# A macaron encoder layer on one core: how the normed input rows are scaled and turned

## The chip, the core and the metric

The kernel runs on one core of a Trainium2 chip. The metric is the device time of one launch in microseconds (us). Engines are named as in the profile: PE (TensorE, with PEld its weight loads), DVE (VectorE), ACT (ScalarE), POOL (GpSimd), SP (SyncE, which here only issues DMAs; ACT issues some too, shown as ACTq).

## The reference, cut to what matters

One layer over 1024 prompt tokens and 32 sample tokens, 1024 features each. The change lies in the first lines, the first feed-forward block:

```
def rms_norm(x, g):
    y = xf * lax.rsqrt(jnp.mean(xf * xf, axis=-1, keepdims=True) + EPS)
    return (y * g.astype(jnp.float32)).astype(x.dtype)

def swiglu(x, w_in, w_out):
    a, b = jnp.split(x @ w_in, 2, axis=-1)
    return (jax.nn.silu(a) * b) @ w_out

x = x + 0.5 * swiglu(rms_norm(x, ffn1_norm), ffn1_w_in, ffn1_w_out)
```

Behind it come the mixing block (stick-breaking attention beside an HGRN2 scan, between two projections) and a second feed-forward block. `d_ff` is 2816, so `ffn1_w_in` is 1024 x 5632. All of it is float32.

## The kernel before, in words

**Products.** A float32 product runs as three products of rounded halves (h and l of each side; `PASSES`, L431). The feed-forward matmuls use a fast scheme of seven block products in place of eight: the normed input, turned so that features lie on partitions, is cut into blocks (`B11`, `B12`, `B21`, `B22`: feature half by token half), and sums of them (`T1` to `T4`) are made. Each block or sum is split into h (ACT, L158) and l (DVE, L159). Tokens come in two column parts, c = 0 (256 columns, operands named `...0h`, `...0l`) and c = 1 (272, in tiles `B11s`, `T2s`). Weights come in 22 column groups j: `load_a(j)` fetches 512 KB (`wraw`, two buffers, so that a load waits until the l of the group two places earlier is written), `load_b(j)` another (`braw`), and S1 to S4 are sums of both.

**The first stage, where the change is.** Nine row tiles (`Tile`: eight of 128 prompt tokens, number 8 with the 32 sample tokens) are fetched in token order (`xt`). For each, `factor` squares the row on ACT with a running sum (L791) and makes the factor r on POOL in two small instructions (L793, L794); before, DVE then makes a 128x128 diagonal `dg` of r (L796). `normed` multiplies the row by that diagonal on PE, eight matmuls per tile (L808), which turns and scales it at once, and DVE multiplies with the gain `g1` out of the PSUM bank (L819, into `xn`). `raw` turns the unscaled row as well (eight transposes with the identity, L806), ACT copies it out (L831), and it goes to DRAM for the residual.

**Order of the work.** Each engine runs its instructions in the order in which a scheduler laid them down at build time from the order of the code and its own estimates; waits are on semaphores. `early_products` runs the products `A11*B11` and `A12*B21` of the groups j = 0 to 5, since they need only two blocks. Its order is j = 0 and 1 for c = 0, then j = 0 and 1 for c = 1, then j = 2, 3, 4, 5 with both parts. After step n it calls `amid(n)`, in which further rows are normed and saved, the remaining operands made (`prep_rest`) and at last the second weights started (`start_weights`: load_a(0) again, load_b(0), the sums on POOL, L479 to L482, and their splits). Then `first_products` runs the other five products of j = 0 (S2*T2 first, in the trace `T20h,S2h`), then j = 1, and so on; partial results of the early products come back from DRAM (`p`, `gt`), and DVE adds the banks up (L552).

Of the kernel before, what the change touches and what calls it, by code (L numbers as in the profile page):

```python
# [45 lines left out]
def first_consts(g, pool, w):  # L46
    nc = g.nc
    tmp = g.wp.tile([P, CW[1]], F32, name="idtmp", tag="xp", bufs=3)[:, 0:P]
    make_identity(nc, tmp)
# [4 lines left out]
    nc.vector.memset(ones, 1.0)
    g.ones = ones[:, 0:1].broadcast_to([P, P])
    g.eps = pool.tile([P, 1], F32, name="eps")
    nc.vector.memset(g.eps, EPS)
    g.g1 = col(g, pool, "g1", w["ffn1_norm"].rearrange("o (c p) -> p (o c)", p=P), KC)
# [717 lines left out]
class Tile:  # L776


    def __init__(self, g, w, pool, psp, tt):
# [4 lines left out]
        tag, bufs = ("xt", 8) if tt < 8 else ("st", 6)
        self.xt = pool.tile([P, D], F32, name="xt", tag=tag, bufs=bufs)
        g.landed = nc.sync.dma_start(self.xt[0:R], src)

    def factor(self, spare):
        g, nc, pool, R = self.g, self.g.nc, self.pool, self.R
        ss = pool.tile([P, 1], F32, name="ss", tag="ss", bufs=3)  # L790
        nc.scalar.activation(spare[0:R], self.xt[0:R], AF.Square, accum_out=ss[0:R])  # L791
        r = pool.tile([P, 1], F32, name="r", tag="r", bufs=3)
        nc.gpsimd.tensor_scalar(out=r[0:R], in0=ss[0:R], scalar1=1.0 / D, scalar2=EPS, op0=ALU.mult, op1=ALU.add)  # L793
        g.power = nc.gpsimd.tensor_tensor(out=r[0:R], in0=r[0:R], in1=g.mh[0:R], op=ALU.pow)  # L794
        self.dg = pool.tile([P, P], F32, name="dg", tag="dg", bufs=4)
        nc.vector.tensor_scalar(out=self.dg[0:R, 0:R], in0=g.ident[0:R, 0:R], scalar1=r[0:R, 0:1], scalar2=None,  # L796
                                op0=ALU.mult)

    def turned(self, h, m):

        nc, R = self.g.nc, self.R
        pn = self.psp.tile([P, 4, P], F32, name="bk", tag="bk", bufs=8)
        for k in range(4):
            src = self.xt[0:R, (4 * h + k) * P:(4 * h + k + 1) * P]
            if m is None:
                nc.tensor.transpose(pn[:, k, 0:R], src, self.g.ident[0:R, 0:R])  # L806
            else:
                nc.tensor.matmul(pn[:, k, 0:R], src, m[0:R, 0:R], start=True, stop=True)  # L808
# [828 lines left out]
def tile_layer(ctx: ExitStack, tc: tile.TileContext, *aps):  # L1637
# [38 lines left out]
    first_consts(g, const, w)  # L1676
# [342 lines left out]
```

## Time and profile before

| | |
|---|---|
| median of three runs | 2153.51 us (2150.92 to 2155.53) |
| profiled execution | 2152.1 us, span of the trace 2150.4 us |
| PE busy | 2106.0 us, 98% of the span |
| DVE, ACT, POOL busy | 1473.9, 938.7, 593.3 us |
| mean granted TensorE clock | 0.998 |

A timeline row reads: start in us, duration in us, engine, line, operation, tile written from tiles read, shapes, how many instructions the row merges, and in brackets how long the engine sat idle before it and what released it. A row of a stage table reads: stretch, its length, busy time (and count) of each engine, PEclk (the TensorE clock that the records show as granted, 1.00 is full), DMA share and GB/s. A DMA row on SPq or ACTq is its issue, not its transfer. L numbers are lines of the kernel before.

### The profile page before, as it was taken

The numbers are of one execution on the slowest core, as the hardware profiler recorded it, in microseconds if no ns is written. First come the engines' busy times: TensorE is split into PE (matmuls) and PEld (weight loads), VectorE is DVE, ScalarE is ACT, GpSimd is POOL, SyncE is SP. The second block draws the span as 40 slices with busy tenths as digits, with TensorE's granted clock in tenths as the row PEclk, the third lists the DMA queues.
The fourth block names the chain that finished last, engine by engine and source line by source line (L and its number), as shares of the span: only waits on it lengthen the run. The fifth ranks groups of instructions, "written<-read, shape, count | busy, mean of one in ns | idle before, by whom it ended". The sixth has DMA issues, their size and how long they took to land.

```text
span 2150.4 us, 41462 instructions
## 1 busy us (share of the span) xinstructions
PE 2106.0 (98%) x16331; PEld 2055.2 (96%) x16331; DVE 1473.9 (69%) x2559; ACT 938.7 (44%) x1830; POOL 593.3 (28%) x873
## 2 busy tenths in 40 slices
PE   7999999999999999999999999999999999999999
PEld 7999999999999999989899898999999999999998
DVE  5877666564678658778778689559777666645775
ACT  6433333233446555555554565236323233334444
POOL 1355544441000110311311311021555354320000
PEclk9999999999999999999999999999999999999999
DMA  7665555547535320120121122464775555566343
GB/s 231 189 211 173 154 175 158 164 137 269 201 124 168 117 62 21 44 71 21 51 63 29 56 66 91 145 196 148 237 219 172 165 166 164 166 222 237 120 148 126
DMA packets 327364, 305.12 MB, mean 142 GB/s; under 512 B 26432, under 2 KB 283200, under 8 KB 327168
## 3 DMA queue, kind: packets, MB, share of 16 engines
q1 hardware_dynamic: 258016, 262.59, 37.8%
q10 hardware_dynamic: 68672, 38.25, 6.2%
q8 instruction: 128, 2.10, 0.4%
q0 software_dynamic: 480, 1.62, 0.2%
q14 instruction: 68, 0.56, 0.1%
HBM read 207.37 MB, written 95.03 MB: 141 GB/s over the span
## 4 chain that ended last, share of the span: by engine, by line
PE 85%; DVE 5%; DMA 4%; issue 2%; POOL 2%; ACT 2%; ACTq 0%; DVEq 0%; SPq 0%; POOLq 0%
PE bk L431 36%; PE bk L752 19%; PE pp L891 14%; PE ps L1529 2%; PE pl L1400 2%; PE av L1167 1%; PE pt L1148 1%; DMA oraw<-in_ffn_w_out_dram 1%; PE z L1203 1%; PE bk L808 1%; PE ps L1556 1%; PE z L1202 1%; DVE t L1061 1%; DMA pd<-e 1%; DMA p<-pd 1%
## 5 line engine op out<-in xcount | busy, mean ns | idle before, releaser
L752 PE MATMUL bk<-tl,wh 128*128 128x256 f32 x1144 | 325.0, 285 | 1.1 <-DVE tl L709 1.1
L752 PE MATMUL bk<-th,wl 128*128 128x256 f32 x1144 | 324.4, 284 | 0.5 <-DVE wl L697 0.5
L752 PE MATMUL bk<-th,wh 128*128 128x256 f32 x1144 | 323.0, 284 | 0.7 <-ACT th L708 0.7
L891 PE MATMUL pp<-xs_a,wh 128*128 128x384 f32 (+1 forms) x1008 | 258.5, 338 | 0.0
L752 PEld LDWEIGHTS bk<-tl,wh 128*128 128x128 f32 x1144 | 215.2, 188 | 1.8 <-DVE tl L709 1.8
L752 PEld LDWEIGHTS bk<-th,wl 128*128 128x128 f32 x1144 | 215.2, 188 | 1.0 <-DVE wl L697 0.7
L752 PEld LDWEIGHTS bk<-th,wh 128*128 128x128 f32 x1144 | 214.4, 188 | 1.2 <-ACT th L708 1.0
L891 PEld LDWEIGHTS pp<-xs_a,wh 128*128 128x128 f32 x1008 | 168.6, 189 | 6.1 <-issue 4.1
L891 PE MATMUL pp<-xs_a,wl 128*128 128x384 f32 (+1 forms) x504 | 163.9, 325 | 0.0
L586 POOL TENSOR_TENSOR gt<-gt,b 128x256 f32<-128x256 f32 x88 | 74.4, 846 | 314.4 <-ACT gt L585 310.3
L697 DVE SCALAR_TENSOR_TENSOR wl<-oraw,wh 128x1024 fp32r<-128x1024 f32 x78 | 89.8, 1152 | 95.8 <-ACT wh L696 95.7
L696 ACT ACTIVATE wh<-oraw 128x1024 fp32r<-128x1024 f32 x78 | 77.7, 996 | 135.4 <-PE bk L752 115.9
L585 ACT ACTIVATE gt<-gt 128x256 f32<-128x256 f32 x88 | 37.3, 424 | 224.2 <-DVE gt L552 224.0
L431 PE MATMUL bk<-ops_a,wh 128*128 128x256 f32 (+1 forms) x704 | 131.6, 287 | 2.5 <-ACT e L411 2.5
L159 DVE TENSOR_TENSOR wl<-wraw,wh 128x512 fp32r<-128x512 f32 (+2 forms) x126 | 110.8, 894 | 33.6 <-ACT wh L158 32.1
L158 ACT ACTIVATE wh<-wraw 128x512 fp32r<-128x512 f32 (+2 forms) x126 | 89.5, 731 | 88.6 <-PE pp L891 25.2
L431 PEld LDWEIGHTS bk<-ops_a,wh 128*128 128x128 f32 x704 | 110.0, 190 | 3.4 <-ACT e L411 3.4
L590 POOL TENSOR_TENSOR gt<-gt,b 128x256 f32<-128x256 f32 x88 | 89.4, 1016 | 80.2 <-DVE b L552 67.8
L431 PE MATMUL bk<-ops_a,wl 128*128 128x272 f32 (+1 forms) x352 | 100.4, 286 | 0.3 <-DVE wl L159 0.3
L552 DVE TENSOR_TENSOR gt<-bk,p 128x256 f32<-128x256 f32 (+1 forms) x60 | 26.0, 433 | 105.9 <-PE bk L431 99.9
L891 PEld LDWEIGHTS pp<-xs_a,wl 128*128 128x128 f32 x504 | 94.7, 188 | 0.1
L1059 ACT ACTIVATE t<-z,minus 128x128 f32<-128x128 f32 (+2 forms) x96 | 55.4, 578 | 63.2 <-PE z L1205 48.9
(446 smaller groups left out, 6701.7 us busy)
## 6 DMA issues: line engine op xcount, KB each, us to landing
wraw<-in_ffn_w_in_dram SPq DMA_DIRECT2D x58, 512.0 KB, 4.3
oraw<-in_ffn_w_out_dram SPq DMA_DIRECT2D x94, 256.0 KB, 4.5
sd<-osum SPq DMA_DIRECT2D x44, 512.0 KB, 3.2
gd<-gt SPq DMA_DIRECT2D x42, 528.0 KB, 5.0
braw<-in_ffn_w_in_dram ACTq DMA_DIRECT2D x42, 512.0 KB, 4.4
oraw<-sd SPq DMA_DIRECT2D x40, 512.0 KB, 3.8
oraw<-in_ffn_w_out_dram SPq DMA_DIRECT2D x30, 512.0 KB, 3.5
wraw<-in_w_in_dram SPq DMA_DIRECT2D x28, 512.0 KB, 3.6
```

Source lines behind the costliest of these rows:

```text
L158: nc.scalar.activation(hi, src, AF.Copy)
L159: return nc.vector.tensor_tensor(out=lo, in0=src, in1=hi, op=ALU.subtract)
L431: mm = g.nc.tensor.matmul(ps, wt[x][:, kk, :], xt[y][:, kk, :], start=(first and kk == 0 and n == 0), stop=(kk == HK - 1 and n == len(PASS ...
L586: nc.gpsimd.tensor_tensor(out=gt[:, 1, cc], in0=gt[:, 1, cc], in1=s["b2"], op=ALU.mult)
L590: last = nc.gpsimd.tensor_tensor(out=gt[:, 0, cc], in0=gt[:, 0, cc], in1=s["b1"], op=ALU.mult)
L696: nc.scalar.activation(h, r, AF.Copy, scale=0.5)
L697: nc.vector.scalar_tensor_tensor(out=l, in0=r, scalar=0.5, in1=h, op0=ALU.mult, op1=ALU.subtract)
L752: nc.tensor.matmul(ps, wt[a][:, d * P:(d + 1) * P], xt[b][:, cols(c)], start=(k == 0 and n == 0), stop=(k == FH - 1 and n == len(PASSES) - 1))
L891: g.filler = nc.tensor.matmul(ps[:, 0:gw(n)], wt[a][:, k, :], xs(b, k)[:, gs(n)], start=(k == 0 and j == 0), stop=(k == KC - 1 and j == le ...
L1059: nc.scalar.activation(a, z, AF.Sigmoid, scale=minus)
L1400: nc.tensor.matmul(pl[0:rows, c, 0:hl].rearrange("p (b m) -> p b m", m=m_), k[:, cs(b, c)][:, 0:rows], qr, start=True, stop=True)
L1529: nc.tensor.matmul(ps[:, 0:w], wt[a][:, k, :], xs(b, c)[:, gs(n)], start=(k == 0 and i == 0), stop=(k == 5 and i == len(PASSES) - 1))
```

## The change

`factor` now multiplies the row itself by r, in two halves of 512 columns, into a new tile `xr`: on ACT for rows 1 and 3, on DVE for rows 0 and 8, on POOL for rows 2, 4, 5, 6 and 7. `normed` turns `xr` with the identity, as `raw` turns `xt`. The diagonals go. Only rows 0 and 1 are turned ahead of the first products; the turns of rows 2, 3 and 8, of 4 and 5, and of 6 and 7 move behind steps 0, 2 and 3. The gain `g1` is fetched behind two row tiles and the first weights, no longer first. `load_a(1)` moves ahead of the first factors in the code.

```
-        self.dg = pool.tile([P, P], F32, name="dg", tag="dg", bufs=4)
-        nc.vector.tensor_scalar(out=self.dg[0:R, 0:R], in0=g.ident[0:R, 0:R], scalar1=r[0:R, 0:1], scalar2=None,
-                                op0=ALU.mult)
+        self.xr = pool.tile([P, D], F32, name="xr", tag="st", bufs=6)
+        for h in range(2):
+            cs = slice(HD * h, HD * h + HD)
+            out, src = self.xr[0:R, cs], self.xt[0:R, cs]
+            if self.tt in (1, 3):
+                nc.scalar.activation(out, src, AF.Copy, scale=r[0:R, 0:1])
+            else:
+                eng = nc.vector if self.tt in (0, 8) else nc.gpsimd
+                eng.tensor_scalar(out=out, in0=src, scalar1=r[0:R, 0:1], scalar2=None, op0=ALU.mult)
...
-            if m is None:
-                nc.tensor.transpose(pn[:, k, 0:R], src, self.g.ident[0:R, 0:R])
-            else:
-                nc.tensor.matmul(pn[:, k, 0:R], src, m[0:R, 0:R], start=True, stop=True)
+            nc.tensor.transpose(pn[:, k, 0:R], rows[0:R, (4 * h + k) * P:(4 * h + k + 1) * P], self.g.ident[0:R, 0:R])
...
     def amid(n):
-        if n == 1:
+        if n == 0:
+            norm_rows(2, 3, 8)
+            factor_rows(4, 5)
+        elif n == 1:
             prep_first(g, None, None, None, xs[1], xns[1])
             save_rows(8, 0, 1)
+            factor_rows(6, 7)
+        elif n == 2:
+            norm_rows(4, 5)
+            save_rows(2)
         elif n == 3:
-            save_rows(2)
-            norm_rows(4, 5)
+            prep_rest(g, None, None, None, xs[0], xns[0])
+            norm_rows(6, 7)
             save_rows(3, 4, 5)
-            for tt in (6, 7):
-                rows[tt].factor(spare)
-            prep_rest(g, None, None, None, xs[0], xns[0])
-            for tt in (6, 7):
-                rows[tt].normed(xns)
+        elif n == 4:
             save_rows(6, 7)
...
     wts.load_a(0)
+    g.g1 = col(g, const, "g1", w["ffn1_norm"].rearrange("o (c p) -> p (o c)", p=P), KC)
     fetch_rows(2, 3, 8)
+    wts.load_a(1)
+    factor_rows(0, 1)
     norm_rows(0, 1)
     wts.split_a(0)
     prep_first(g, None, None, None, xs[0], xns[0])
-    wts.load_a(1)
-    norm_rows(2, 3, 8)
+    factor_rows(2, 3, 8)
```

The scheduler lays the instructions down anew. Line numbers of the changed kernel differ: its L789 is L791 of before, L791 and L792 are L793 and L794, L157 and L158 are L158 and L159, L451 and L459 are L452 and L460, L551 is L552, L430 is L431; its L798 and L801 are the new multiplications.

ACT at the start of the program, before: squares of the rows (`T40h` is only scratch there), the first weights' h, and the h of the first two blocks.

```order
2 L791 ACTIVATE T40h,ss<-xt 128x1024 x2
3 L158 ACTIVATE wh<-wraw 128x1024
4 L791 ACTIVATE T40h,ss<-xt 128x1024 x2
5 L791 ACTIVATE T40h,ss<-xt 32x1024
6 L158 ACTIVATE B110h<-xn_104 128x1024
7 L158 ACTIVATE B210h<-xn_104 128x1024
8 L158 ACTIVATE wh<-wraw 128x1024
```

ACT at the same place, changed:

```order
2 L789 ACTIVATE T40h,ss<-xt 128x1024 x2
3 L157 ACTIVATE wh<-wraw 128x1024
4 L798 ACTIVATE xr<-xt,r 128x512 x2
5 L789 ACTIVATE T40h,ss<-xt 128x1024 x2
6 L798 ACTIVATE xr<-xt,r 128x512
7 L157 ACTIVATE B110h<-xn_88 128x1024
8 L157 ACTIVATE B210h<-xn_88 128x1024
9 L798 ACTIVATE xr<-xt,r 128x512
10 L789 ACTIVATE T40h,ss<-xt 32x1024
```

The multiplications of row 1 stand ahead of the squares of rows 2 and 3, and the first half of row 3's stands ahead of `B110h`. The factor that it waits for comes from POOL, which at the start of the changed kernel runs this row (rows 0 and 1, then row 2 with its multiplications, then row 3, then row 8):

```order
9 L791 TENSOR_SCALAR r<-ss 128x1 x2
10 L792 TENSOR_TENSOR r<-r,mh 128x1 x2
11 L791 TENSOR_SCALAR r<-ss 128x1
12 L792 TENSOR_TENSOR r<-r,mh 128x1
13 L801 TENSOR_SCALAR xr<-xt,r 128x512 x2
14 L791 TENSOR_SCALAR r<-ss 128x1
15 L792 TENSOR_TENSOR r<-r,mh 128x1
16 L791 TENSOR_SCALAR r<-ss 32x1
17 L792 TENSOR_TENSOR r<-r,mh 32x1
```

Row 3's factor now stands behind both multiplications of row 2; before, POOL had only the pairs of small instructions.

SP's DMA issues from the third weight load on, before: three more weight loads (j = 3, 4, 5), then `braw` of j = 0, then three (j = 0 again, 1, 2).

```order
8 L452 DMA wraw<-in_ffn_w_in_dram 128x8x128
9 L786 DMA xt<-in_x_prompt_dram 128x1024 x2
10 L452 DMA wraw<-in_ffn_w_in_dram 128x8x128 x3
11 L460 DMA braw<-in_ffn_w_in_dram 128x8x128
12 L452 DMA wraw<-in_ffn_w_in_dram 128x8x128 x3
```

The same place, changed:

```order
8 L451 DMA wraw<-in_ffn_w_in_dram 128x8x128
9 L784 DMA xt<-in_x_prompt_dram 128x1024 x2
10 L451 DMA wraw<-in_ffn_w_in_dram 128x8x128 x5
11 L459 DMA braw<-in_ffn_w_in_dram 128x8x128
12 L451 DMA wraw<-in_ffn_w_in_dram 128x8x128
```

`braw` of j = 0 now stands behind five loads, the last two of which are those of j = 0 and 1 for the second time.

DVE at the end of j = 0 in `first_products`, before (`u` is the first addition for j = 1 and needs the `p` that comes from DRAM; `S4l` is a weight of j = 1):

```order
82 L552 TENSOR_TENSOR b_1137<-bk,p_1117 128x272
83 L159 TENSOR_TENSOR A22l<-braw,A22h 128x512
84 L552 TENSOR_TENSOR gt_953<-bk,u_1090 128x272
85 L552 TENSOR_TENSOR u_1185<-bk,p_1167 128x256
86 L159 TENSOR_TENSOR S4l<-rS_1030,S4h 128x512
```

And changed:

```order
73 L551 TENSOR_TENSOR b_1146<-bk,p_1126 128x272
74 L158 TENSOR_TENSOR A22l<-braw,A22h 128x512
75 L551 TENSOR_TENSOR gt_962<-bk,u_1099 128x272
76 L158 TENSOR_TENSOR S4l<-rS_1039,S4h 128x512
77 L551 TENSOR_TENSOR u_1194<-bk,p_1176 128x256
```

`S4l` has come ahead of the `u` that waits for `p`. From j = 4 of `first_products` on, all engines run the same instructions in the same order in both kernels.

More of the change, by code (lines that the diff above doesn't have):

```diff
@@ L57, in first_consts @@
     nc.vector.memset(g.eps, EPS)
-    g.g1 = col(g, pool, "g1", w["ffn1_norm"].rearrange("o (c p) -> p (o c)", p=P), KC)
     g.r = pool.tile([P, T], F32, name="rstd")
@@ L783, in __init__ @@
         R = self.R
-        tag, bufs = ("xt", 8) if tt < 8 else ("st", 6)
-        self.xt = pool.tile([P, D], F32, name="xt", tag=tag, bufs=bufs)
+        self.xt = pool.tile([P, D], F32, name="xt", tag="xt", bufs=9)
         g.landed = nc.sync.dma_start(self.xt[0:R], src)
@@ L789, in factor, with turned @@
         g, nc, pool, R = self.g, self.g.nc, self.pool, self.R
-        ss = pool.tile([P, 1], F32, name="ss", tag="ss", bufs=3)
+        ss = pool.tile([P, 1], F32, name="ss", tag="ss", bufs=9)
         nc.scalar.activation(spare[0:R], self.xt[0:R], AF.Square, accum_out=ss[0:R])
-        r = pool.tile([P, 1], F32, name="r", tag="r", bufs=3)
+        r = pool.tile([P, 1], F32, name="r", tag="r", bufs=9)
         nc.gpsimd.tensor_scalar(out=r[0:R], in0=ss[0:R], scalar1=1.0 / D, scalar2=EPS, op0=ALU.mult, op1=ALU.add)
         g.power = nc.gpsimd.tensor_tensor(out=r[0:R], in0=r[0:R], in1=g.mh[0:R], op=ALU.pow)
-        self.dg = pool.tile([P, P], F32, name="dg", tag="dg", bufs=4)
-        nc.vector.tensor_scalar(out=self.dg[0:R, 0:R], in0=g.ident[0:R, 0:R], scalar1=r[0:R, 0:1], scalar2=None,
-                                op0=ALU.mult)
-    def turned(self, h, m):
+        self.xr = pool.tile([P, D], F32, name="xr", tag="st", bufs=6)
[7 more added lines that the diff above has]
+                eng.tensor_scalar(out=out, in0=src, scalar1=r[0:R, 0:1], scalar2=None, op0=ALU.mult)
+    def turned(self, h, rows):
         nc, R = self.g.nc, self.R
@@ L813, in normed @@
         for h in range(2):
-            pn = self.turned(h, self.dg)
+            pn = self.turned(h, self.xr)
             ks = slice(4 * h, 4 * h + 4)
@@ L830, in raw @@
         for h in range(2):
-            nc.scalar.activation(st[:, 4 * h:4 * h + 4, 0:R], self.turned(h, None), AF.Copy)
+            nc.scalar.activation(st[:, 4 * h:4 * h + 4, 0:R], self.turned(h, self.xt), AF.Copy)
         if tt < 8:
@@ L1675, in tile_layer @@
     g.wp = ctx.enter_context(tc.tile_pool(name="wp", bufs=2, reuse_waits="tile"))
-    first_consts(g, const, w)
     g.slabs = Slabs(g, g.wp, slabs_of(w["w_in"], mix_cols)
@@ L1702, in fetch_rows, with factor_rows @@
             rows[tt] = Tile(g, w, ldp, psp, tt)
+    fetch_rows(0, 1)
+    first_consts(g, const, w)
+    def factor_rows(*tts):
+        for tt in tts:
+            rows[tt].factor(spare)
     def norm_rows(*tts):
         for tt in tts:
-            rows[tt].factor(spare)
             rows[tt].normed(xns)
@@ L1713, in amid @@
     def amid(n):
-        if n == 1:
+        if n == 0:
+            norm_rows(2, 3, 8)
+            factor_rows(4, 5)
+        elif n == 1:
             prep_first(g, None, None, None, xs[1], xns[1])
             save_rows(8, 0, 1)
+            factor_rows(6, 7)
+        elif n == 2:
+            norm_rows(4, 5)
+            save_rows(2)
         elif n == 3:
-            save_rows(2)
-            norm_rows(4, 5)
+            prep_rest(g, None, None, None, xs[0], xns[0])
+            norm_rows(6, 7)
             save_rows(3, 4, 5)
-            for tt in (6, 7):
-                rows[tt].factor(spare)
-            prep_rest(g, None, None, None, xs[0], xns[0])
-            for tt in (6, 7):
-                rows[tt].normed(xns)
+        elif n == 4:
             save_rows(6, 7)
```

2 lines of the change are left out of this document (removed).

## The prediction

> **What bounds the kernel now.** I read first the stages, cut where PE's work changes: before the first matmul, the first turns, the first products with the rest of the turns, the early products of j = 2 to 5, the first two groups of the full products, and the rest.
>
> ```profile
> 0.00:7.67 7.67, 0.00 (x0) 0.00 (x0) 0.64 (x5) 3.56 (x5) 1.45 (x8) 1.00 0.73 223
> 7.67:19.74 12.07, 12.06 (x80) 11.91 (x80) 9.17 (x15) 9.78 (x15) 3.90 (x11) 1.00 0.96 348
> 19.74:52.45 32.71, 28.68 (x233) 28.13 (x233) 19.21 (x32) 18.65 (x34) 3.30 (x6) 0.95 0.72 199
> 52.45:75.87 23.42, 23.42 (x195) 23.42 (x194) 21.92 (x27) 14.43 (x24) 5.60 (x3) 1.00 0.54 165
> 75.87:111.19 35.32, 31.47 (x242) 30.86 (x241) 26.34 (x46) 11.69 (x23) 17.42 (x17) 0.95 0.62 193
> 111.19:2150.00 2038.81, 2010.37 (x15589) 1960.87 (x15587) 1396.66 (x2439) 880.55 (x1733) 561.60 (x828) 1.00 0.43 138
> ```
>
> The first number behind the comma is PE's busy time. From 111.19 on PE is the bound, and the order there is nearly the same in both kernels, so what is gained or lost by that point is gained or lost at the end. The whole question is when PE reaches the third group (j = 2), at 111.2 before. Ahead of it stand PE's own turns (7.67 to 19.74) and two stretches with 4 us of idle PE each. Second, PE's timeline:
>
> ```profile
> 7.68 12.14 PE L808 MATMUL bk<-dg,xt 128*128 128x128 f32 x80 [7.68 <-DVE dg L796]
> 19.75 0.39 PE L431 MATMUL bk<-B110h,wh 128*128 128x256 f32 x1
> 34.89 3.74 PE L808 MATMUL bk<-dg,xt 128*128 128x128 f32 x32
> 38.46 2.78 PE L806 MATMUL bk<-identr,xt 128*128 128x128 f32 x24
> 41.90 2.02 PE L808 MATMUL bk<-dg,xt 128*128 128x128 f32 x16 [0.66 <-PE bk L806]
> 47.30 3.32 PE L808 MATMUL bk<-dg,xt 128*128 128x128 f32 x16 [3.37 <-ACT B220h L158]
> 50.41 2.29 PE L806 MATMUL bk<-identr,xt 128*128 128x128 f32 x16
> 75.88 0.28 PE L431 MATMUL bk<-T20h,S2h 128*128 128x256 f32 x1
> ```
>
> A diagonal matmul is two passes (80 for five rows, 16 each), a plain turn is one. Third, the clock, by PE's pace and by PEclk:
>
> ```profile
> 7.67:13.64 5.97, 5.96 (x28) 5.96 (x29) 1.00 1.08 377
> 13.64:19.74 6.10, 6.10 (x54) 5.94 (x53) 1.00 0.85 318
> 52.45:75.87 23.42, 23.41 (x192) 23.42 (x193) 1.00 0.54 165
> 37.53:40.95 3.42, 3.42 (x33) 1.00 0.63 178
> 40.95:44.36 3.41, 2.32 (x19) 1.00 0.84 255
> 44.36:47.77 3.41, 0.47 (x4) 1.00 0.95 243
> 47.77:51.18 3.41, 3.41 (x18) 0.50 1.18 293
> 98.97:102.38 3.41, 1.48 (x12) 1.00 1.04 356
> 102.38:105.80 3.42, 3.42 (x17) 0.50 0.85 254
> ```
>
> The first two lines are L808 alone, the third L431 alone: 0.213 us a pass at first, 0.113 us from 13.64 on, so the first 6 us ran at half clock although PEclk says 1.00 there. The clock changes on a grid of 3.41 us. A stretch with PE busy 1.48 of 3.41 us or less is followed by one at half clock; 2.32 was enough to stay. A product costs 0.122 us (192 in 23.42) at full clock and 0.201 (17 in 3.42) at half.
>
> **The change part by part.** *The start.* Before, the blocks' last half `B210l` is ready at 18.24 and PE is still turning until 19.75. Now PE turns two rows, is done near 12 us and waits for `B110h`. On ACT that stands behind the first half of row 3's multiplication, which waits for row 3's factor on POOL, which stands behind row 2's two multiplications there.
>
> ```profile
> 10.97 1.06 ACT L791 ACTIVATE T40h<-xt 128x1024 fp32r<-128x1024 f32 x1 [0.46 <-DMA xt<-in_x_prompt_dram]
> 10.60 0.19 POOL L793 TENSOR_SCALAR r<-ss 128x1 f32<-128x1 f32 x1 [1.98 <-ACT T40h L791]
> 10.87 0.55 POOL L794 TENSOR_TENSOR r<-r,mh 128x1 f32<-128x1 f32 x1
> 13.98 1.06 ACT L158 ACTIVATE B110h<-xn 128x1024 fp32r<-128x1024 f32 x1 [0.64 <-DVE xn L819]
> 17.02 1.22 DVE L159 TENSOR_TENSOR B210l<-xn,B210h 128x1024 fp32r<-128x1024 f32 x1
> 48.70 1.27 POOL L479 TENSOR_TENSOR rS<-braw 128x512 f32<-128x512 f32 x1 [1.83 <-issue]
> 65.18 2.66 POOL L480 TENSOR_TENSOR rS<-rS,wraw 128x512 f32<-128x512 f32 x1 [15.21 <-DMA wraw<-in_ffn_w_in_dram]
> ```
>
> Row 2's square ends at about 10.9 as before (its DMA sets it; row 1's two halves on ACT fit ahead of it), and its factor is there 0.9 us later, at 11.8. A POOL multiplication of 128x512 by a column is not in the trace. Below stands the same operation on one column, 0.19; above, two-input operations of that shape, 1.27 with DVE idle and 2.66 with DVE at work. I take 0.8, nearer to 1.27, since the shape is the same but one input falls away. Two make 13.4, row 3's factor 0.8 more (14.2), ACT's half 0.6, `B110h` 1.06 (15.9), DVE's `B110l` 1.22: the products run from 17.1 on, two of them and two turns already done (0.4), as if from 16.7. Gain 3.0; by 0.19 and 2.66 it is 4.2 and -0.7. The Trainium skill's GPSIMD Engine Reference (Engine selection) says that one-input elementwise work there is about line rate; its 1.03 cycles an element make an estimated 0.44 us and a gain of 3.7, and no row here shows it.
>
> *The clock.* PE stands still for some 4 us ahead of these products, so they begin at half clock, for one to two grid steps: 5.1 us at 0.201 instead of 0.122 lose 2.0 (1.3 to 2.7). Before, this time fell on the diagonals.
>
> *Turns behind the first products.* Before, rows 4 to 7 took 64 passes at 0.112, 7.2 us. Now they are 32 turns at 0.109 (24 in 2.6 us), 3.5, and the 24 turns of rows 2, 3 and 8 come in as well, 2.2. Gain 1.5. The raw turns stay.
>
> *The stop at 41 to 52.* Rows 6 and 7 got their factors late, since their squares stood on ACT behind copies: 0.8 us ahead of 41.90, 3.4 ahead of 47.30, and 1.7 for the half clock of 47.77 to 51.18. Now the squares stand ahead of the copies, ten or more us before the turns that need them. Gain 5.9. In exchange POOL's last multiplication meets DVE's two-input subtractions, and DVE's splits of j = 4 end only just ahead of their products: I put 0.5 for both (0 to 1.5).
>
> *Costless.* The diagonals (0.28 us each) and the multiplications of rows 0 and 8 on DVE hide behind DMA and ACT; `g1` is needed two us after it can land, and its fetch no longer delays row 0 (half a us, inside the start's chain). Without that cover each would cost its own duration.
>
> By here PE reaches S2*T2 7.9 us earlier, at 68.0. What is late next:
>
> ```profile
> 59.92 1.28 DVE L159 TENSOR_TENSOR wl<-wraw,wh 128x512 fp32r<-128x512 f32 x2
> 65.41 1.28 DVE L159 TENSOR_TENSOR wl<-wraw,wh 128x512 fp32r<-128x512 f32 x2
> 43.39 0.37 SPq L460 DMA_DIRECT2D braw<-in_ffn_w_in_dram  x1
> braw<-in_ffn_w_in_dram SPq DMA_DIRECT2D x1, 512.0 KB, 5.2
> 79.44 1.29 DVE L159 TENSOR_TENSOR T2s<-xn,T2s 128x1088 fp32r<-128x1088 f32 x1 [0.40 <-ACT T2s L158]
> 80.76 0.34 SPq L557 DMA_DIRECT2D p<-pd  x1
> 84.51 0.44 DVE u L552
> 91.20 0.87 DVE L159 TENSOR_TENSOR S2l<-rS,S2h 128x512 fp32r<-128x512 f32 x1
> 92.12 0.39 PE L431 MATMUL bk<-T20h,S2l 128*128 128x256 f32 x1 [1.29 <-DVE S2l L159]
> 100.91 0.39 PE L431 MATMUL bk<-B220h,S4l 128*128 128x256 f32 x1 [2.51 <-DVE S4l L159]
> ```
>
> *The wait for braw.* Its load was issued at 43.39, 32 us ahead of S2*T2. Now it stands on SP behind the second load for j = 1, which needs the buffer that the split of j = 5 frees (66.69 before, 9.2 us ahead of S2*T2). From that split's end: 0.45 for the issue in front, 5.2 to land, POOL's S1 1.27, S2 about 2.0 (1.3 to 2.66), S3 1.3, ACT's h 0.6: S3h after 10.8, where PE, after four products of S2 and S1, wants it at 9.7. The split itself comes about 1 us later against PE, since a copy now lies between its ACT halves. Loss 2.1 (0.5 to 3.5).
>
> *The group j = 1.* DVE's five splits of S and A22 now come behind that wait and ahead of three of the `T2s` splits. When the last `T2s` is done, the `p` load may start (80.76 behind 80.73). Before, that was 4.9 us behind PE's start of S2*T2, now some 9; `u` and all behind it, up to `S2l` of j = 1, follow 4 us later against PE: a wait of about 4 us and probably a grid step at half clock, 1.4. Before, this place lost 1.5 (ahead of 92.12), 2.7 (ahead of 100.91) and 1.4 (102.38 to 105.80). The 2.7 go, because `S4l` no longer stands behind the `u` that waits for `p`. Net 0 (-3 to +4).
>
> Sum: 3.0 - 2.0 + 1.5 + 5.9 - 0.5 - 2.1 + 0 = 5.8. Against the profiled 2152.1 that gives 2146.3; its execution lay 1.4 under the median of the runs, and half of that added gives 2147.0.
>
> **The rivals.** *The new waits do not come* (braw lands in time, DVE keeps up): 2.1 more, and some 3.5 of the 5.6 lost at j = 1 with them, gain 11.4, 2141.5. For it: DVE has 13 us of idle time in 19.74 to 52.45; against it: 1.5 us in 52.45 to 75.87. *The start eats it*: POOL's multiplications at 1.3 to 2.66, two full grid steps at half clock, and a third one at S2*T2, gain 0 to 3, 2151. For it: DVE works beside POOL, and POOL went from 1.3 to 2.66 so; against it: ahead of `B110h` DVE mostly reads PSUM. *Slower: the clock stays down.* If a grid step counts as busy only without turns, the early products stay at half clock as long as turns are strewn among them. Each us so costs about 0.43; the gain is gone with 13 us more of it than I count, near 35 us. Did it hold until the last raw turns ahead of j = 2's second part, 118 products lose 0.079 and 110 turns about 0.1 each, 20 us, of which 2.0 are counted and some 4 come back as waits saved: slower by 8, 2160. The rows speak against it: 37.53 to 40.95 was turns from 38.46 on, and the clock stayed up behind it. The Trainium skill's page TensorE: Matmul & The Clock Gate (PE-mode transpose) has that rule: transposes do not count as PE-busy in the same way. The trace does not bear it out. *The diagonals might stay*: the order excludes it, every L808 row now reads the identity.
>
> **How the numbers follow.** Forecast 0.52 (own range 2144 to 2150), no new waits 0.20, the start eats it 0.20, slower 0.05, other 0.03. Telling from no change needs 0.2%, 4.3 us, so below 2149.2 is faster: 0.75 of the forecast (0.39), all of the first rival, 0.03 of the rest, 0.62. Same: 0.13, 0.17 and 0.01, 0.31. Slower 0.07. The range 2141.5 to 2151.5 runs from the first rival to the second; the ends of the unknown costs lie in it.
>
> **What would show it.** First large run of products near 17 us, at 0.2 us each until 20 to 24. No PE gap over 1 us between 22 and 66. S2*T2 reached near 68, with a gap at S2h or S3h and `braw` issued near 60. A gap of some 4 us at j = 1, none at `S4l`. S2*T2 of j = 2 near 105. It would be wrong if PE's products began behind 19, if gaps appear at turns that wait for POOL, or if `braw` lands before 62.

## The result, and the profile after

| | before | changed |
|---|---|---|
| median | 2152.55 us (6 runs, 2149.74 to 2155.53) | 2171.81 us (5 runs, 2171.55 to 2173.89) |
| profiled execution, its span | 2152.1, 2150.4 us | 2173.89, 2172.2 us |
| ratio | | 1.009, 95% interval 1.0078 to 1.0102 |

A sixth run of the changed kernel, at 2542.34 us with a granted clock of 0.754, is left out of its median and of the ratio. The change made the kernel 0.9% slower, 19.3 us, where 2147.0 had been forecast. The profiled executions stand 21.8 us apart, and the following marks, read from PE's timeline, say where these lie. The last column sets the forecast's own marks against the trace (75.9 - 7.9 for the first, 111.2 - 5.8 for the second, unchanged from there).

| PE reaches | before | changed | later by | new in this stretch | later than forecast, new in this stretch |
|---|---|---|---|---|---|
| S2*T2 of j = 0 | 75.9 | 78.1 | 2.2 | 2.2 | 10.1 |
| S2*T2 of j = 2 | 111.2 | 118.5 | 7.3 | 5.1 | 3.0 |
| S2*T2 of j = 6 | 174.8 | 192.1 | 17.3 | 10.0 | 10.0 |
| first product of the second feed-forward block | 1455.5 | 1474.1 | 18.6 | 1.3 | 1.3 |
| end | 2150.4 | 2172.2 | 21.8 | 3.2 | 3.2 |

The changed kernel by stages, cut at the same events (stretch; its length; busy time and count of PE, PEld, DVE, ACT, POOL; PEclk; DMA share; GB/s):

```profile
8.24:19.81 11.57, 3.68 (x16) 3.28 (x16) 4.00 (x7) 5.99 (x10) 4.62 (x6) 1.00 0.98 354
19.81:52.45 32.64, 31.04 (x248) 29.55 (x249) 27.13 (x39) 22.08 (x39) 16.47 (x18) 1.00 0.49 136
52.45:78.09 25.64, 21.77 (x171) 20.69 (x169) 14.31 (x15) 12.90 (x22) 4.19 (x3) 1.00 0.72 206
78.09:118.53 40.44, 35.57 (x240) 33.60 (x241) 28.92 (x44) 12.99 (x23) 15.82 (x15) 0.87 0.51 156
118.53:192.09 73.56, 65.69 (x504) 64.46 (x505) 51.38 (x94) 20.96 (x41) 41.02 (x45) 0.95 0.65 201
192.09:2170.00 1977.91, 1949.30 (x15085) 1900.10 (x15084) 1351.43 (x2355) 861.12 (x1697) 527.28 (x789) 1.00 0.42 136
```

And the kernel before, over the groups j = 2 to 5:

```profile
111.19:174.79 63.60, 61.73 (x506) 61.15 (x505) 46.64 (x86) 18.36 (x36) 37.59 (x40) 1.00 0.71 214
```

The largest single loss is in a stage whose instructions the change moves little: 504 matmuls take 73.56 us where 506 took 63.60. Of the 10.0 us, 6.0 are idle time of PE (7.87 against 1.87), and 4.0 are slower passes, with the clock at 0.95 in place of 1.00. In the stage ahead of it, 4.1 of the 5.1 us are slower passes (35.57 us busy against 31.47), at 0.87 in place of 0.95; the first stretch at half clock (0.21 us a pass until 85.5) comes right behind the waits at S2*T2.

The start of the changed kernel, from the first block's factors to the first run of products:

```profile
7.70 0.88 DVE L801 TENSOR_SCALAR xr<-xt,r 128x512 f32<-128x512 f32 x2 [6.08 <-POOL r L792]
11.85 1.06 ACT L789 ACTIVATE T40h<-xt 128x1024 fp32r<-128x1024 f32 x1 [1.64 <-DMA xt<-in_x_prompt_dram]
14.01 3.12 POOL L801 TENSOR_SCALAR xr<-xt,r 128x512 f32<-128x512 f32 x2
18.09 0.72 ACT L798 ACTIVATE xr<-xt,r 128x512 f32<-128x512 f32 x1 [3.78 <-POOL r L792]
18.72 1.04 ACT L157 ACTIVATE B110h<-xn 128x1024 fp32r<-128x1024 f32 x1
19.79 1.23 DVE L158 TENSOR_TENSOR B110l<-xn,B110h 128x1024 fp32r<-128x1024 f32 x1 [7.14 <-ACT B110h L157]
21.42 0.56 PE L430 MATMUL bk<-B110l,wh 128*128 128x256 f32 x1
```

Row 2's square starts at 11.85 when its DMA lands (9.36 before). On SP the same four loads stand ahead of row 2 in both kernels, but now `g1` stands right in front of it; it took 6.1 us to land (2.3 before), and SP's issue of row 2 itself took 3.58 us. No run moves `g1` alone, so this cause is not shown. In the nine traces whose start is that of the changed kernel the square starts at 9.6 to 11.9, and the run of products at 19.2 to 21.4. POOL needs 1.56 us for each half of row 2, and row 3's factor, ACT's half, `B110h` and `B110l` follow one after the other.

PE's idle time from there to S2*T2 (groups by line and tiles: count, busy, mean ns, idle before and its releasers; then the whole stretch as a stage row):

```profile
L430 PE MATMUL bk<-B11s,wh 128*128 128x272 f32 x96 | 19.1, 295 | 2.0 <-ACT e L410 1.6 <-DVE e L412 0.4
L808 PE MATMUL bk<-identr,xt 128*128 128x128 f32 (+1 forms) x72 | 8.9, 270 | 1.2 <-DVE e L412 1.0 <-DVE xn L819 0.2
L430 PE MATMUL bk<-T20h,S2h 128*128 128x256 f32 x1 | 0.4, 387 | 1.8 <-ACT S2h L157 1.8
```

```profile
24.28:78.09 53.81, 48.70 (x401) 46.44 (x399) 38.12 (x49) 31.35 (x55) 19.94 (x19) 1.00 0.64 180
```

`e` are the copies of early products out of PSUM banks on their way to DRAM (`pd`): where PE waits for one, it waits for a free bank. In all PE stands idle for 5.1 of 53.81 us.

Behind S2*T2, the chain of waits of the changed kernel (start, us, what) leads to the first `p` load:

```profile
81.89 0.48 ACTq L414
82.41 5.87 DMA pd<-e
88.50 0.42 DVE e L412
88.93 1.40 DVE T2s L158 x2
91.36 3.78 DMA p<-pd
```

A store of `e` issued late on ACT's queue holds a buffer until 88.3; DVE's next `e` copy waits for that buffer, the last `T2s` splits stand behind it on DVE, and the `p` load behind them. It is issued 13.3 us behind PE's start of S2*T2; before, 4.9.

Now the view that the forecast had not asked for: the chain of waits of the kernel *before*, by line, for 111 to 161 us and for 161 to 200:

```profile
by line: DMA oraw<-in_ffn_w_out_dram 25.4%; issue 17.0%; DMA wraw<-in_ffn_w_in_dram 9.8%; POOL gt L586 9.2%; POOL osum L529 6.1%; DMA braw<-in_ffn_w_in_dram 6.0%; POOL osum L531 4.9%; POOL osum L530 4.5%; DVE b L552 4.3%; POOL osum L532 4.1
...
by line: PE bk L431 98.0%; DVE A22l L159 1.6%; DVE b L552 0.9%; issue 0.1%
```

PE was busy for 61.73 of 63.60 us from 111.19 on, and yet it is not among the ten largest parts of this chain until 161. There the chain runs through a loop that keeps almost the same pace as PE: `p` load, `u` and the further sums on DVE, POOL's products with `gt` and, in order with them, its sums `osum`, which wait for `oraw` from DRAM, the stores `td` and `sd`, and on SP behind those the next `p` load, which also needs its buffer back. A group's pace in it is read from the issues of the loads (tile `p` on SP, 75 to 205 us: durations ns min/median/max, first and last start; who waited for it: us, times), before and changed:

```profile
L557 SPq DMA_DIRECT2D p<-pd x12: 319/341/548, 80.8 to 166.7; - x12
...
  DVE u L552: 12.2, 8
```

```profile
L556 SPq DMA_DIRECT2D p<-pd x12: 319/338/1102, 91.4 to 184.4; - x12
...
  DVE u L551: 21.3, 6
```

The first load is 10.6 us later, the twelfth 17.7; from first to last it is 93.0 us in place of 85.9. Of the 7.1, 4.7 arise in one turn. For c = 0 the loads go at 80.8, 95.6, 111.5, 126.6, 141.9 and 161.2 before, and at 91.4, 106.4, 127.0, 142.8, 158.5 and 178.4 now: the turn from j = 1 to j = 2 takes 20.6 us instead of 15.9. SP ahead of the load of j = 1, before and changed:

```profile
92.69 0.37 SPq L533 DMA_DIRECT2D sd<-osum  x1
...
95.07 0.39 SPq L452 DMA_DIRECT2D wraw<-in_ffn_w_in_dram  x1
95.61 0.51 SPq L557 DMA_DIRECT2D p<-pd  x1
...
99.83 0.43 DVE L552 TENSOR_TENSOR u<-bk,p 128x256 f32<-128x256 f32 x1 [3.30 <-DMA p<-pd]
```

```profile
105.38 0.37 SPq L532 DMA_DIRECT2D sd<-osum  x1
105.84 0.46 SPq L451 DMA_DIRECT2D wraw<-in_ffn_w_in_dram  x1
106.40 1.10 SPq L556 DMA_DIRECT2D p<-pd  x1
...
113.48 0.42 DVE L551 TENSOR_TENSOR u<-bk,p 128x256 f32<-128x256 f32 x1 [5.44 <-DMA p<-pd]
```

Before, `sd` (512 KB) left 2.9 us ahead of `p`, with `td` and `wraw` between them. Now `td` comes first, and `sd`, `wraw` (512 KB each) and `p` are issued within 1.1 us; `u` starts 7.1 us after the issue, 4.2 before. All kernels below that have either half of the change and keep the loop show this order and a long turn there (17.6 us or more).

### The profile page after: what moved, and what is told of

Same layout as the page of the kernel before. It is cut to its first block, busy times and chain, and to the rows that moved or that the text cites. A ratio compares the mean times of both kernels' runs of the same rounds, so it can differ in the third digit from the quotient of the medians.

```text
span 2172.2 us, 41332 instructions
## 1 busy us (share of the span) xinstructions
PE 2107.0 (97%) x16259; PEld 2051.7 (94%) x16259; DVE 1478.1 (68%) x2554; ACT 939.9 (43%) x1834; POOL 611.6 (28%) x883
## 4 chain that ended last, share of the span: by engine, by line
PE 79%; DVE 7%; DMA 6%; ACT 2%; issue 2%; POOL 2%; ACTq 0%; SPq 0%; DVEq 0%; POOLq 0%
PE bk L430 33%; PE bk L751 19%; PE pp L891 14%; PE ps L1529 2%; PE pl L1400 2%; DMA p<-pd 1%; PE av L1167 1%; PE pt L1148 1%; DMA pd<-e 1%; DMA oraw<-in_ffn_w_out_dram 1%; PE z L1203 1%; DVE t L1061 1%; PE ps L1556 1%; PE z L1202 1%; PE pb L243 1%
## 5 line engine op out<-in xcount | busy, mean ns | idle before, releaser
L158 DVE TENSOR_TENSOR wl<-wraw,wh 128x512 fp32r<-128x512 f32 (+2 forms) x126 | 110.8, 894 | 36.1 <-ACT wh L157 34.4
L430 PE MATMUL bk<-ops_a,wh 128*128 128x256 f32 (+1 forms) x704 | 130.0, 285 | 1.7 <-ACT e L410 1.7
L157 ACT ACTIVATE wh<-wraw 128x512 fp32r<-128x512 f32 (+2 forms) x126 | 89.5, 731 | 84.8 <-PE pp L891 25.2
L430 PEld LDWEIGHTS bk<-ops_a,wh 128*128 128x128 f32 x704 | 108.8, 188 | 2.1 <-ACT e L410 1.9
L430 PE MATMUL bk<-ops_a,wl 128*128 128x272 f32 (+1 forms) x352 | 99.9, 284 | 0.4 <-DVE wl L158 0.3
L551 DVE TENSOR_TENSOR gt<-bk,p 128x256 f32<-128x256 f32 (+1 forms) x60 | 25.9, 432 | 96.8 <-PE bk L430 89.3
L551 DVE TENSOR_TENSOR u<-bk,p 128x256 f32<-128x256 f32 x88 | 37.5, 426 | 67.7 <-DMA p<-pd 40.3
```

What stands on the lines that cost most here:

```text
L157: nc.scalar.activation(hi, src, AF.Copy)
L158: return nc.vector.tensor_tensor(out=lo, in0=src, in1=hi, op=ALU.subtract)
L430: mm = g.nc.tensor.matmul(ps, wt[x][:, kk, :], xt[y][:, kk, :], start=(first and kk == 0 and n == 0), stop=(kk == HK - 1 and n == len(PASS ...
L551: add = lambda out, other: nc.vector.tensor_tensor(out=out, in0=ps, in1=other, op=ALU.add)
```

## The experiments

Two profiles of kernels with the same code up to a mark differ by some 3 us in it: the six with all of the changed kernel's first stage have their first `p` at 88.3 to 91.4, the four with that of before at 79.2 to 80.8. Marks are read with that in mind; the times are medians, and the ratios are against the kernel before on the same chip. The edits are cut to the lines that matter.

**Which half of the change.** `mult_alone` is the kernel before with multiplied rows and plain turns; `move_alone` is the changed kernel with diagonals.

```
mult_alone (against before)
-                nc.tensor.matmul(pn[:, k, 0:R], src, m[0:R, 0:R], start=True, stop=True)
+            nc.tensor.transpose(pn[:, k, 0:R], rows[0:R, ...], self.g.ident[0:R, 0:R])
move_alone (against changed)
-                eng.tensor_scalar(out=out, in0=src, scalar1=r[0:R, 0:1], scalar2=None, op0=ALU.mult)
+        nc.vector.tensor_scalar(out=self.dg[0:R, 0:R], in0=g.ident[0:R, 0:R], scalar1=r[0:R, 0:1], ...)
```

> The kernel before with the multiplied rows and plain turns, but every square, factor and turn where it stood before. Feeding theory (the loss comes from what the moved work puts late: braw, the T2s splits, then the loop of the first groups): the rows alone cost little, S2*T2 of j = 0 is reached between 73 and 79 us and the time is 2146 to 2160. Start theory (POOL's multiplications at 1.56 us each and ACT's row 3 in front of B110h are the bulk of the loss): first long run of products at 22 or later, S2*T2 3 to 6 us later than before (79 to 82), time 2157 to 2170.

> The changed kernel with the diagonals back (two passes a turn, no multiplied rows); all squares, factors, turns and stores where the change puts them. Feeding theory: most of the loss stays, braw is still issued behind 60 us and T2s of j = 0 split behind 68 us, time 2163 to 2175. Start theory: most of the loss goes, products run from 17 to 18 us, time 2148 to 2158.

Measured: 2172.46 us, ratio 1.0086 [1.007, 1.0102], and 2164.27, 1.0044 [1.0029, 1.0059]. Each half alone is slower, and the two don't add up: by the ratios 18.5 and 9.5 us for the halves, 19.4 for both. The time of `mult_alone` lies above both forecasts. S2*T2 of j = 0 comes at 76.2 and 75.0, about as before (75.9), but the first `p` at 88.0 and 84.7, and from first to twelfth they take 93.6 and 93.0 us, like the changed kernel. So the loss is not in what the halves do to PE ahead of S2*T2; either makes the first `p` late, and what follows is alike; whether that is the loop is the next question.

**Is it the loop?** The buffer of `p` is handed to the sum `u3`, so the next `p` waits until `u3` has been read. In `after_u3` and `before_u3` that sum overwrites `u2` instead, which has no later reader.

```
-                    s["b2"], s["u3"] = tmp("b2"), tmp("p1")
+                    s["b2"], s["u3"] = tmp("b2"), s["u2"]
```

> The changed kernel, with u3 written over u2 instead of into p1's buffer, so that p may be loaded as soon as the half before has added its p (some 3 us earlier in each half), in both feed-forward layers. Loop theory (in the first groups p, u, the sums, the td store and the next p form a loop of 15.1 to 20 us a turn, against 14.55 of PE; what the first p is late is never made good): the turns of p fall to PE's 14.6 to 15, PE reaches S2*T2 of j = 6 at 180 to 187 instead of 192.1 and the second layer loses 3 to 6 us too; time 2155 to 2165. Rival (PE is held by the feeding of each group itself, T2s and S splits, and by half clock): under 3 us gained.

> The kernel before, with the same edit (u3 over u2). Loop theory: before runs the loop at 15.1 to 15.3 us a turn, 0.6 above PE's 14.55; 1 to 3 us are gained over the groups j = 2 to 5, and 2 to 6 in the second layer (groups at 14.6 instead of 15.1); time 2144 to 2150. Rival: nothing moves, 2152 to 2155.

Measured: 2164.3 us, 1.0054 [1.0039, 1.0069], and 2152.09, 0.9993 [0.9984, 1.0003]. The same view of `p`, first the changed kernel with the edit, then the kernel before with it:

```profile
L556 SPq DMA_DIRECT2D p<-pd x12: 320/339/534, 90.2 to 171.3; - x12
...
  DVE u L551: 5.1, 2
```

```profile
L557 SPq DMA_DIRECT2D p<-pd x12: 319/340/423, 79.9 to 160.7; - x12
...
  DVE u L552: 2.9, 3
```

One line, with nothing of the change undone, takes the changed kernel's eleven steps from 93.0 to 81.1 us, DVE's wait for `p` from 21.3 to 5.1, and the ratio from 1.009 to 1.0054, some 8 us. From S2*T2 of j = 2 to that of j = 6 PE now takes 65.5 us at a clock of 1.00, where the changed kernel took 73.6 at 0.95. In the kernel before the steps go from 85.9 to 80.8 and the time stays, where the loop theory had forecast 2144 to 2150: its loop was close enough to PE's pace to cost nothing that can be measured. The loop is shown as a cause; 11 us are left. With the edit, `p` of j = 1 also leaves ahead of `sd` and `wraw` (101.98 against 104.53 and 104.99), so the wait for the buffer and the place in SP's queue are undone together.

**The order at j = 1.** `oraw_first` puts the two `oraw` loads of that place ahead of `td` and `p` on SP.

```
+            if between is not None and (j, c) == (1, 0):
+                with behind(g, last, stored):
+                    raw = out_loads(g, post, w_out, *halves[n_out])
...
+            with behind(g, g.oraw_in if raw is not None else None):
                 store.dma_start(td[:, j // FH, j % FH, cc], tt)
```

> The changed kernel, with the two oraw loads of j = 1 put back ahead of the td store and of the p load on the SP queue, where they stood before the change. Loop theory: the turn of p from j = 1 to j = 2 falls from 20.6 to 16 to 17 us, PE reaches j = 3 and all behind it 3.5 to 4.7 us earlier; time 2166 to 2169. Rival (the order on SP does not matter, DVE's lateness does): under 1 us.

Measured: 2173.3 us, 1.0101 [1.0083, 1.0118]. The turn still takes 20.0 us (106.1 to 126.1), and `u` still starts 7.2 behind `p`'s issue. The `oraw` loads are not its cause. That `sd`, `wraw` and `p` go out together remains as what the trace shows there; `td` and `sd` were not swapped alone.

**What makes the first p late?** `braw_first` fetches `braw` of j = 0 ahead of the second load of j = 0; `before_late_braw` does the reverse to the kernel before. `rows23_dve` multiplies rows 2 and 3 on DVE. `stores_first` and `stores_ahead` save the raw rows earlier, since `T2s` lies in memory that the last of them frees.

```
braw_first (against changed)
+            wts.pool = a1
+            wts.load_b(0, True)
             wts.lay_out(a1)
before_late_braw (against before)
-        wts.load_a(0)
-        wts.load_b(0)
+        landed = wts.load_a(0)
+        with behind(g, landed if wts.late else None):
+            wts.load_b(0)
rows23_dve (against changed)
-            if self.tt in (1, 3):
+            if self.tt in (1,):
-                eng = nc.vector if self.tt in (0, 8) else nc.gpsimd
+                eng = nc.vector if self.tt in (0, 2, 3, 8) else nc.gpsimd
stores_first (against changed; stores_ahead has the same rows under high priority)
-            save_rows(3, 4, 5)
-        elif n == 4:
-            save_rows(6, 7)
+            save_rows(3, 4, 5, 6, 7)
```

> The changed kernel, with the load of braw for j = 0 issued ahead of the second fetch of the first a-half (0') instead of behind it and its successor, into the first buffer that comes free. Feeding theory with braw as the larger part: S2h is ready by 70, PE reaches S2*T2 at 71 to 74 instead of 78.1, the two half-clock steps of 78.9 to 85.7 go, and 5 to 10 us are gained at the end (2162 to 2167). Feeding theory with T2s as the larger part: S2*T2 is earlier by 4 to 6, but the last T2s split still ends near 88 to 91, so the p load and all later groups stay and the end moves by less than 3. Start theory: less than 2 at the end.

> The kernel before, with one edge added: braw of j = 0 is loaded behind the second fetch of the first a-half on SP, where the slower kernels have it. SP's queue is otherwise the same; some 10 rows of splits change places on ACT and DVE with it. Theory that the late braw is the larger part of the first layer's loss: braw issued at 60 to 64, POOL's sums behind 65, the first p load at 85 to 88 instead of 79.2 to 80.8, the first S2*T2 of j = 6 at 180 to 186 instead of 174.2 to 174.8, time 2158 to 2165. Rival (T2s is held back by the late raw stores and squares on ACT, braw is beside it): p at 80 to 82, time 2151 to 2156.

Measured: 2170.6 us, 1.0077 [1.0059, 1.0096], and 2153.69, 1.0008 [0.9999, 1.0017]. The issue of `braw`, changed, `braw_first`, `before_late_braw`:

```profile
66.69 0.78 SPq L459 DMA_DIRECT2D braw<-in_ffn_w_in_dram  x1
```

```profile
60.45 0.37 SPq L463 DMA_DIRECT2D braw<-in_ffn_w_in_dram  x1
69.59 1.11 ACT L157 ACTIVATE T2s<-xn 128x1088 fp32r<-128x1088 f32 x1 [7.14 <-DMA pd<-e]
```

```profile
58.87 0.53 SPq L463 DMA_DIRECT2D braw<-in_ffn_w_in_dram  x1
```

With `braw` issued 6.2 us sooner, S2*T2 still comes at 78.6: PE now waits there for `S2h`, which stands on ACT behind copies and a `T2s` that waits 7.14 for a store of `e`. The first `p` comes at 84.5, but the steps to the twelfth take 93.5. In this trace the second block begins 5.1 us sooner than in the changed kernel, but then takes 700.2 us in place of 698.1, and the interval of the ratio holds that of the changed kernel. In the kernel before, a `braw` 15.5 us later cost nothing that can be told from none (in the changed kernel it is 23.3 later). The late `braw` is one of several things that hold S2*T2, and by itself it decides nothing.

> The changed kernel with rows 2 and 3 multiplied on DVE instead of POOL and ACT, so that B110h no longer stands behind row 3 on ACT and row 3's factor not behind row 2's two multiplications (1.56 us each) on POOL. Start term of the prediction: the long run of products begins at 16.5 to 18 instead of 21.4. Loop theory: what counts at the end is the first p load, which waits for the last T2s split; with PE, ACT and DVE 3 to 4 us earlier up to there it is issued at 87 to 89 instead of 91.4 and the end moves by 2 to 5 (2167 to 2170). Start theory (the start is the bulk of the loss): 8 or more gained.

Measured: 2171.39 us, 1.0088 [1.0072, 1.0103]. The run of products begins at 17.8 (19.2 to 21.4 with the changed kernel's start), S2*T2 at 74.2, the first `p` at 87.2, the twelfth at 179.7 (92.5 for the steps), and the ratio stays that of the changed kernel. The start is slower than forecast, but alone it is not why the kernel is slower.

> The changed kernel, with the raw turns and stores of rows 6 and 7 one step earlier (as before the change), so that the memory of T2s comes free before the splits of j = 4 and 5. Feeding theory with T2s as the larger part: the first T2s split starts near 60 to 64 instead of 71.1, the last ends near 84 to 87 instead of 91.3, p is issued then, S2*T2 itself stays near 78 (braw), and 4 to 10 us are gained at the end. With braw as the larger part: under 3 gained. Start theory: under 2.

> The changed kernel with all raw copies and stores of rows 3 to 7 given priority, so that on ACT they stand ahead of the splits of j = 4 and 5 (the run stores_first moved them in the program but not on ACT: its last store was issued at 65.2 against 66.0). Theory that the late raw stores hold back the memory of T2s and the p load: last store issued by 52 to 56, the first p load at 83 to 88 instead of 91.4, 3 to 8 us gained at the end (2164 to 2169). Rival (DVE's and ACT's order of S and T2s splits, behind the late braw, sets the first p load): p stays at 90 to 92 and the end within 2 of the changed kernel.

Measured: 2177.66 us, 1.0103 [1.0086, 1.012], and 2172.49, 1.0091 [1.0074, 1.0108]. In the first the last row's store still left at 65.21 us (65.98 in the changed kernel, 56.00 before), since ACT kept it behind splits of weights, so it tests nothing. In the second it left sooner, but `T2s` then stood behind the splits of S, and the first `p` came at 90.4. Late stores alone are not the cause.

**The second feed-forward block.** It runs the same instructions in the same order, yet took 698.1 us in place of 694.9. One theory was that PE's instruction fetches (one of 16 KB in about 128 matmuls) had moved against the `p` loads, since the change takes 72 matmul records away. The five kernels add matmuls that nothing reads, to move the fetches: `fetch_shift_after`, `fetch_after` and `phase_after` to the changed kernel, `fetch_before` and `phase_before` to the kernel before.

```
+    extra = psp.tile([P, 512], F32, name="bk", tag="bk", bufs=8)
+    for i in range(28):
+        nc.tensor.matmul(extra[:, 0:32], g.ident, g.ident[:, 0:32], start=(i == 0), stop=(i == 27), ...)
```

(28 in `phase_before`, 56 in `fetch_before`, 36 in `phase_after`, 72 in `fetch_after`, all between the first and the second product of the first block; 72 in `fetch_shift_after`, ahead of the second block.)

> The changed kernel with 72 matmuls of 128x32 on the identity ahead of the second layer's first product, so that the number of instructions that PE has issued there is that of the kernel before (16331 matmuls). They cost some 4 to 9 us of PE's own time (read from the trace and taken off). Fetch theory (the second layer's extra 3 to 5 us come from the 16 KB fetches of PE's instructions, one in 128 matmuls, which in the changed kernel fall on the p load of each group, 1.3 us behind its issue, and in the kernel before 7 us behind it): from S2*T2 of j = 0 to the end of the first groups (j = 8) the second layer is 3 to 5 us shorter than in the changed kernel, its turns of p are 15.1 to 15.4 instead of 15.6 to 16.3, and no fetch falls within 3 us behind a p load. Rival (the state in which the layer begins, DVE's lateness, sets it): turns as in the changed kernel, 15.6 to 16.3.

> The kernel before with 56 more matmuls (128x32, accumulated into one bank) between the first layer's first and second products; nothing else moves on any engine. From there on PE has issued as many instructions, counted in fetches of 128 matmuls, as in the changed kernel. Their own time (2 to 6 us) is read from the trace. Fetch theory (the second layer's extra 3 us come from where PE's 16 KB fetches fall against the p loads of its first groups): from the second layer's first product to the end 693 to 695 us instead of 690.4, fetches 0 to 3 us behind several p loads, turns of p 15.6 to 16.3. Rival (the second layer's length follows from something else, such as the state in which it begins): 689.5 to 691.5.

> The changed kernel with 72 more matmuls at the same place, which brings the count of fetches to that of the kernel before; nothing else moves. Fetch theory: from the second layer's first product to the end 690 to 691.5 instead of 693.5, fetches 6 to 9 us behind the p loads, turns of p 15.1 to 15.4. Rival: 693 to 694.

> The kernel before with 28 added matmuls of two passes each (56 records) between the first layer's first and second products, nothing else moved: the phase of PE's fetches (one in 128 matmuls) in the second layer is that of the changed kernel. Fetch theory: second layer, from its first product to the end, 693 to 696 us instead of 690.4. Rival: 689 to 691.5. The added passes themselves cost some 10 us.

> The changed kernel with 36 added matmuls of two passes each (72 records) at the same place: the phase is that of the kernel before. Fetch theory: second layer 689 to 691.5 us instead of 693.5. Rival: 693 to 696. The added passes themselves cost some 13 us.

Measured: 2208.9 us, 1.0262; 2169.77, 1.008 [1.0065, 1.0095]; 2199.08, 1.0215 [1.0199, 1.023]; 2162.78, 1.0054 [1.0039, 1.0069]; 2181.23, 1.0142 [1.0123, 1.0162]. Each such matmul appears as two passes, so that the first three shifted by twice the number meant, and cost 20 to 27 us themselves. The last two were made with half. The second block's first product (PE's timeline) in before, changed, `phase_before` and `phase_after`, whose spans end at 2150.4, 2172.2, 2159.9 and 2182.1:

```profile
1455.47 0.59 PE L431 MATMUL bk<-ops_a,wh 128*128 128x256 f32 x2
```

```profile
1474.08 0.60 PE L430 MATMUL bk<-ops_a,wh 128*128 128x256 f32 x2
```

```profile
1462.19 0.60 PE L431 MATMUL bk<-ops_a,wh 128*128 128x256 f32 x2
```

```profile
1483.95 0.60 PE L430 MATMUL bk<-ops_a,wh 128*128 128x256 f32 x2
```

The kernel before got 697.7 us, 2.8 more, as the theory had it; the changed one kept 698.2 where it had wanted some 695. One of two directions is no proof. What can be said is that the block takes 693.5 to 695.8 us in seven of the eighteen traces, and 697.4 to 700.2 in ten (`fetch_shift_after` has 707.1); all three with `u3` over `u2` are among the seven. With the loop kept and no matmul added, the three kernels with 16331 matmul records take 694.6 to 695.8 and the seven with 16259 take 697.4 to 700.2; `phase_after` was brought back to 16331 and keeps 698.2, so the count alone does not decide it. Why it goes the one way or the other stays open.

**All three together.** `all_mended` is the changed kernel with the edits of `braw_first`, `after_u3` and `rows23_dve`.

> The changed kernel with braw first, u3 over u2, and rows 2 and 3 multiplied on DVE. Loop theory: the three parts act at different places (first p load earlier by 5 to 8, turns at PE's 14.6 to 15.5, start earlier by 4): S2*T2 of j = 6 at 172 to 180 instead of 188.7 to 192.1, time 2150 to 2160; if it falls below 2152 it beats both. Rival (they remove the same wait three times): the gain is that of the best one alone, 182 to 186, time 2162 to 2166.

Measured: 2150.19 us (10 runs, 2147.48 to 2152.07) against 2151.81, ratio 0.9994 [0.9984, 1.0004]. Its `p`:

```profile
L563 SPq DMA_DIRECT2D p<-pd x12: 319/337/1342, 83.2 to 162.1; - x12
...
  DVE u L558: 0.7, 1
```

S2*T2 of j = 6 comes at 173.6 (192.1 in the changed kernel), DVE's wait for `p` is 0.7 us, and the second block takes 693.5. The single edits had brought that mark to 182.8, 185.9 and 187.4; taken from the mean of four profiles with the changed first stage (190.7), that is 7.9, 4.8 and 3.3, 16.0 in all, and 17.1 came; the last two lie near the scatter of the four (188.7 to 192.1). S2*T2 of j = 0 itself comes at 77.4, hardly sooner than the changed kernel's 78.1, so the gain lies behind it. Together the edits bring the kernel some 20 us under the changed one, which is all that the change had lost, and no more: the version equals the kernel before and can't be told faster. Pairs of the edits were not run.

## Why the prediction was wrong, step by step

The sum's 2146.3 for a profiled execution missed by 27.6 us: 10.1 ahead of S2*T2, 3.0 in j = 0 and 1, 10.0 in j = 2 to 5, 4.5 behind.

*"From 111.19 on PE is the bound."* This step failed, and with it the rule that what is gained by then is gained at the end: 10.0 us more were lost in j = 2 to 5, where the forecast had put nothing. It was taken from PE's busy share. The chain over the same time names DVE, POOL, SP's loads and DMA until 161; what counts there is when the first `p` leaves, and how long the steps behind it take.

*"The group j = 1: net 0 (-3 to +4)."* The text saw that the first `p` moves behind the `T2s` splits, 9 us behind S2*T2 instead of 4.9; it was 13.3, since a store of `e` came between. But it counted this as one wait of PE, made good at the next place. In the loop it is not made good, and the turn at j = 1 adds 4.7 us to it.

*"Gain 3.0 at the start (4.2 to -0.7)."* It lost: the run of products began at 21.4 and not 17.1. Row 2's square ended at 12.9 where the text had 10.9 "as before", because its load came later (2.0; the move of `g1`, now right in front of it, had been put at nothing, and in other traces with this start the square ends as early as 10.7); POOL's two multiplications took 3.12 and not 1.6 (1.5); the hand-overs took the rest. The forecast had 0.8 a multiplication, nearer to the lower of its bounds 0.19 and 2.66; measured, 1.56, and that with DVE idle (from 12.6 to 19.8), so the choice between its bounds by DVE's work was not what mattered. By the Trainium skill's GPSIMD Engine Reference (Engine selection) such one-input work runs at about line rate, an estimated 0.44 us; the trace does not bear it out. For its size this miss mattered little, as `rows23_dve` shows.

*The clock: -2.0.* Right in kind: half clock until 24.28, some 1.3 us lost, the lower bound. Of the half clock behind S2*T2 (0.87 in place of 0.95 until j = 2, 0.95 in place of 1.00 from there) the forecast had counted one step of 1.4, at j = 1. The rival in which strewn turns keep the clock down fell: PEclk is 1.00 from 24.28 to 78.09 with 126 turns strewn in. The Trainium skill's rule on transposes (TensorE: Matmul & The Clock Gate, PE-mode transpose) is not borne out by that row.

*Turns behind the products.* Right in kind: they ran at 0.10 to 0.11 us each. Turns and products of this stretch together took 1.8 us more than the rows by which they were priced.

*"The stop at 41 to 52: gain 5.9, less 0.5."* Both stops went (of the 5.9 us, the row at 41.90 shows 0.66 and not the 0.8 that was added up), but 5.1 us of new ones came, where 0.5 was set: 3.0 for banks whose `e` copies were late on ACT and DVE, 1.8 for `S2h`, the rest short. The mark "no PE gap over 1 us between 22 and 66" failed at 51.2 (1.04). These engines had taken the copies, squares and multiplications into the time in which the banks had been emptied before. Start, half clock, stops and dearer passes are 4.3 - 0.7 + 4.6 + 1.8 = 10.0 of the 10.1 us.

*The wait for braw: -2.1.* Its size was about right (`braw` issued 11.4 us ahead of S2*T2, waits of 1.8 there and 1.3 at the next two, which the profile puts down to `e` copies), but taking it away in `braw_first` brought no PE time, because other work on ACT held `S2h` then.

*The rivals.* The slower one put forward was the clock. The mechanism that did decide, a loop through DVE, POOL, SP and DRAM with a period close to PE's, was not among them, and "slower" had 0.07.

## What to carry to other kernels

Before a forecast says "from here on this engine is the bound", read the chain of waits for that window alone: 97% busy did not mean that PE alone set the pace. Where a load's buffer is handed on to a sum, a loop through memory runs beside the bound with a period of its own; here it was about as long as PE's, and a late first turn was not made good. Such a buffer is a good first thing to change: here it cost one line and gave some 8 us. An edit that fills the idle time of helper engines should be costed by the queue it makes on them: what stood behind that idle time (bank copies, stores, the load that starts the loop) comes late.

## What the runs showed of the hardware

POOL took 1.56 us or a little more (1.72 at most, ten times) for a 128x512 multiplication by a column, with DVE idle too, beside 0.48 on DVE (0.88 for two in a row) and 0.72 on ACT for the same shape. A `p` load issued right behind two transfers of 512 KB from the same queue was there some 7 us after its issue, where 3.2 is the median. A matmul of plain float32 with 32 columns was recorded as two passes and took 0.24 us (28 in 6.8, mean granted clock 0.89) to 0.36 us (56 in 20.1, at 0.60). Instruction fetches have a DMA queue of their own (changed kernel; packets, MB, share):

```profile
q8 instruction: 127, 2.08, 0.4%
```

That is 16 KB for each 128 of the 16259 matmuls; by the share each took about 1 us.
